# Modulating the first slice beside half of x, and summing two modulation vectors on VectorE from slice 3 on

## The chip, the core and the metric

The kernel runs on one core of one Trainium2 chip. The core has TensorE (PE in the profile; its weight loads are PEld), VectorE (DVE), ScalarE (ACT), GpSimd (POOL) and SyncE (SP), each with its own queue of instructions in order, and 16 DMA engines that all queues share. The metric is the device time of one execution in microseconds. Before the change its median is 1101.84 us in 3 runs (1101.22 to 1101.95).

## What is computed

One decoder block for 512 tokens of width 1024: a projection of the modulated and normalised input to gates, a spatial-gating branch and a Mamba-2 branch, then an output projection and an MLP. The change touches only the beginning, cut here to what matters:

```python
mod = (silu(c) @ w_mod + b_mod)          # one row of 6*1024
sh1, sc1, g1, sh2, sc2, g2 = split(mod, 6)
h = rms_norm(x) * (1.0 + sc1) + sh1      # 512 x 1024
proj = h @ w_in                          # 512 x 10272
u, v, z, xbc, dt_raw, gate_a, gate_b = split(proj, offs)
```

## The kernel before

All arithmetic is float32. A large product is three products of float32r halves: each operand is split into a rounded part H and a remainder L, and HH, HL and LH are summed in PSUM. One product of a 128x128 stationary tile with 128x512 moving columns is called a matmul below. ScalarE writes the H of a weight (a cast), VectorE the L (a subtraction).

h is kept transposed (channels in partitions, tokens in columns) in eight slices of 128 channels, slice k in hH[k] and hL[k]. The first stage is a loop over the slices (L420): as soon as slice k is there, its 896 columns of w_in (384 of u, 512 of v) are multiplied with it into seven PSUM banks that stay open for the whole loop: vps[0..3], one for each block of 128 tokens, and ups[0..2]. One slice takes 21 matmuls, three kinds (HH, HL, LH) for seven banks. The rest of the program, 14 times as long, follows: v's second half (v1), u, gates, the two branches, the output and the MLP.

What a slice needs ahead of that:

- **x** is loaded in eight halves of 128 tokens by 512 channels (xt[t][0] and xt[t][1]; in listings of the order of instructions x_66 to x_73, in the order t=0 first half, t=0 second half, t=1 first half, and so on). xstat(t) (L359) sums the squares of the two halves, one on ScalarE and one on VectorE; xn(t) (L371) scales 256 channels by 1/rms and transposes two slices' blocks on TensorE. For later slices xn_t (L349) transposes four blocks, and ScalarE copies them out of PSUM (xnT).
- **sh1 and 1+sc1 of the slice** come from mod_load(k) (L230), two loads of 512 KB on SyncE's queue, then mod_rows(k) (L312), eight small TensorE products of silu(c) with them, a copy to SBUF (mrow), mod_cols(k) (L323), two transposes and a reduction, and an addition of the bias. The result is mcol[k] (mc in the profile).
- **the modulation** writes hH[k] on ScalarE (mod_H, L377) and the same in float32 on GpSimd, for k=0 on VectorE (mod_f, L380); VectorE subtracts them to hL[k] (low, L107).
- **w_in's 896 columns** are loaded by start_load(k) (L247) and split by start_H and start_L (L341, L345).

Buffers set when loads may start: three for mod (rawt), four for w (wide). spin(n) (L272) is n matmuls of ones that nobody reads. There are two rings of PSUM banks, five "mm" and three "sx"; after the open banks have been given out one sx bank is left, which mod_rows, mod_cols and xn_t share in turn.

The engine order is that of the code for PE, ACT, DVE and SP in this stage (class InOrder). In the loop mod_rows(k+1) stands after the second of slice k's matmuls, mod_cols(k+1) after the seventh, xn_t(k+2) after the thirteenth:

```python
if n == (7 if k == 0 else 1) and k + 1 < KB:
    mod_rows(k + 1)
if n == (12 if k == 0 else 6) and k + 1 < KB:
    mod_cols(k + 1)
```

After the loop GpSimd issues loads of small vectors in a block that waits for pool_at (L454): dcol (d_skip), bsb (gm_bs) and wsr (gm_ws), used from vectors() (L515) and spatial() (L573) on.

Of the kernel before, what the change touches and what calls it, by code (L numbers as in the profile page):

```python
# [10 lines left out]
AF = mybir.ActivationFunctionType  # L11
ALU = mybir.AluOpType
# [3 lines left out]
P = 128  # L16
S = 512
D = 1024
NT = S // P
KB = D // P  # L20
# [3 lines left out]
MASKED = -30000.0  # L24
OU, OV, OZ, OX, OB, OC, ODT, OGA, OGB = 0, 1024, 2048, 4096, 6144, 7168, 8192, 8224, 9248
AHEAD = 2
SPIN = 16
POOL_L = {("ga", 0), ("ga", 1), ("gm", 0), ("ga", 2), ("wo", 1, 0), ("wo", 1, 1), ("f1", 0, 0), ("f1", 0, 1)}
NB = 43

# [2 lines left out]
def hybrid_block(ctx: ExitStack, tc: tile.TileContext, x, c, w_mod, b_mod, w_in, gm_norm_w, gm_ws,  # L33
# [3 lines left out]
    pool = nc.gpsimd  # L37
# [20 lines left out]
    pe, dve, act = InOrder(nc.tensor, True), InOrder(nc.vector, True), InOrder(nc.scalar, True)  # L58
    sp = InOrder(nc.sync, True)
# [15 lines left out]
    def blk(name, dt=F32, n=512):  # L75
        return big.tile([P, n], dt, tag="b", name=nm(name), bufs=NB)

    def small(name, n):
        return big.tile([P, n], F32, tag="sm", name=nm(name), bufs=16)

    def wide(name):
        return big.tile([P, 1024], F32, tag="cr", name=nm(name), bufs=4)
# [18 lines left out]
    def add(o, a, b):  # L101
        dve.tensor_tensor(o, in0=a, in1=b, op=ALU.add)

    def stt(o, a, s, b, op0, op1):
        dve.scalar_tensor_tensor(o, in0=a, scalar=s, in1=b, op0=op0, op1=op1)

    def low(L, src, H, eng=None):  # L107
        (eng or dve).tensor_tensor(L, in0=src, in1=H.bitcast(F32), op=ALU.subtract)  # L108
# [7 lines left out]
    mm, tr = pe.matmul, pe.transpose  # L116
# [71 lines left out]
    W = w_in[0]  # L188
# [32 lines left out]
    xt = [[blk("x"), blk("x")] for _ in range(NT)]  # L221

    def x_load(eng, t, j):
        eng.dma_start(xt[t][j], x[0, t * P:(t + 1) * P, j * 512:(j + 1) * 512])
# [9 lines left out]
            sp.dma_start(raw[:, j], w_mod[0][:, c0:c0 + P].rearrange("(k p) n -> p k n", p=P))  # L234
        return raw

    for t in range(NT):
        x_load(act, t, 0)
    x_load(sp, 0, 1)
    x_load(sp, 1, 1)  # L240
    sp.dma_start(crow, c.rearrange("a (r p) -> (a r) p", p=P))
    modraw = [mod_load(0)]
    x_load(sp, 2, 1)
    x_load(sp, 3, 1)
    C0 = OU + 640

    def start_load(k):  # L247
        raw = wide("w0")
        sp.dma_start(raw[:, 0:896], W[k * P:(k + 1) * P, C0:C0 + 896])
        return raw  # L250

    startraw = [start_load(0)]
    for k in range(1, KB):
        modraw.append(mod_load(k))
        startraw.append(start_load(k))
# [1 line left out]
    ones = const([P, P], "ones")  # L257
    dve.memset(ones, 1.0)
    ident = const([P, P], "ident")
# [12 lines left out]
    def spin(n):  # L272
        for _ in range(n):
            mm(spinps[:, 0:P], lhsT=ones, rhs=ones, start=True, stop=True)
# [22 lines left out]
    cact = const([P, KB], "cact")  # L297
# [6 lines left out]
    bm = const([P, KB, 2], "bm")  # L304
# [29 lines left out]
    def wide_pair(name):
        pair = [big.tile([P, KB, S], F32R, tag=f"hh{i}", name=nm(name), bufs=1) for i in range(2)]
        return pair, [pair[0][:, k, :] for k in range(KB)], [pair[1][:, k, :] for k in range(KB)]

    _, hH, hL = wide_pair("h")
    wstart = {}

    def start_H(k):  # L341
        wstart[k] = whl()
        act.copy(wstart[k][0][:, 0:896], startraw[k][:, 0:896])

    def start_L(k):  # L345
# [11 lines left out]
    rs = [small("rstd", 1) for _ in range(NT)]  # L357

    def xstat(t):  # L359
        sqacc(accx[t][:, 0:1], xt[t][0])  # L360
        dve.scalar_tensor_tensor(blk("junk"), in0=xt[t][1], scalar=1.0, in1=xt[t][1], op0=ALU.mult, op1=ALU.mult,
                                 accum_out=accx[t][:, 1:2])
        add(ssx[t], accx[t][:, 0:1], accx[t][:, 1:2])
        act.activation(sqx[t], ssx[t], AF.Sqrt, bias=epsc, scale=1.0 / D)

    def xscale(eng, t, c0, c1):
        o = xt[t][c0 // 512]
        eng.tensor_scalar(o[:, c0 % 512:c0 % 512 + c1 - c0], in0=o[:, c0 % 512:c0 % 512 + c1 - c0], scalar1=rs[t],
                          scalar2=None, op0=ALU.mult)

    def xn(t):  # L371
        dve.reciprocal(rs[t], sqx[t])
        xscale(dve, t, 0, 256)
        for k in range(2):
            xn_t(tps[k], k, t)

    def mod_H(k, xk, t0=0, t1=S):  # L377
        act.activation(hH[k][:, t0:t1], xk[:, t0:t1], AF.Identity, bias=mcol[k][:, 0:1], scale=mcol[k][:, 1:2])

    def mod_f(k, xk):  # L380
        hf = blk("h")
        at = (pool if k else dve).tensor_scalar(hf, in0=xk, scalar1=mcol[k][:, 1:2], scalar2=mcol[k][:, 0:1],
                                                op0=ALU.mult, op1=ALU.add)
        return hf, at.ins

    xstat(0)
    xstat(1)
# [1 line left out]
    xn(0)  # L389
    spin(3)  # L390
    xn(1)
    spin(6)
    mod_rows(0)
    spin(2)
    xstat(2)
    mod_cols(0)
    xscale(dve, 0, 256, 512)
    spin(2)
    xn(2)
    xscale(dve, 1, 256, 512)  # L400
    mod_H(0, tps[0], 0, 256)
    spin(4)
    xstat(3)
    wstart[0] = whl()
    pool.tensor_copy(wstart[0][0][:, 0:896], startraw[0][:, 0:896])
    xn(3)
    mod_H(0, tps[0], 256, 512)
    hf, _ = mod_f(0, tps[0])
    low(hL[0], hf, hH[0])
    act.copy(xnT[1], tps[1])  # L410
    start_L(0)
    for t in (0, 1, 2, 3):
        act.mul(xt[t][1], xt[t][1], rs[t])
    for t in (2, 3):
        xscale(dve, t, 256, 512)
    start_H(1)
    start_L(1)
    vps = [mm_bank() for _ in range(NT)]
    ups = [mm_bank(), sx_bank(), sx_bank()]
    for k in range(KB):  # L420
        WH, WL = wstart[k]
        H, L = hH[k], hL[k]
        banks = [(vps[t], t) for t in range(NT)] + [(ps, 4 + j) for j, ps in enumerate(ups)]
        steps = [(i, b) for i in range(3) for b in banks] if k < KB - 1 else [(i, b) for b in banks for i in range(3)]
        for n, (i, (ps, b)) in enumerate(steps):
            w, h = (WL if i == 2 else WH), (L if i == 1 else H)
            if b < 4:
                lhsT, rhs = h[:, b * P:(b + 1) * P], w[:, 384:896]
            else:
                lhsT, rhs = w[:, (b - 4) * P:(b - 3) * P], h  # L430
            mm(ps, lhsT=lhsT, rhs=rhs, start=k == 0 and i == 0, stop=k == KB - 1 and i == 2)
            if n == (7 if k == 0 else 1) and k + 1 < KB:
                mod_rows(k + 1)
            if n == (12 if k == 0 else 6) and k + 1 < KB:
                mod_cols(k + 1)
            if n == (17 if k == 0 else 12) and k + 2 < KB:
                tp = sx_bank()
                for t in range(NT):
                    xn_t(tp, k + 2, t)
        if k + 1 < KB:  # L440
            mod_H(k + 1, xnT[k + 1])
            hf, pool_at = mod_f(k + 1, xnT[k + 1])
        if k + 2 < KB:
            act.copy(xnT[k + 2], tp)
            start_H(k + 2)
        if k + 1 < KB:
            low(hL[k + 1], hf, hH[k + 1])
        if k + 2 < KB:
            start_L(k + 2)

    dve.on = act.on = sp.on = False

# [36 lines left out]
    vps = [mm_bank() for _ in range(NT)]  # L489
# [571 lines left out]
```

## Time and profile before

| what | value |
|---|---|
| median of 3 runs | 1101.84 us (1101.22 to 1101.95) |
| the profiled execution | 1104.26 us |
| its span, first to last instruction | 1102.6 us |
| TensorE busy | 1080.4 us, 98% of the span |
| VectorE, ScalarE, GpSimd busy | 642.1, 479.0, 192.8 us |
| first matmul of slice 0 | 20.69 us |
| first matmul of slice 1, of slice 7, of v1 | 29.27, 69.09, 73.85 us |

Times in the trace count from the span's start. The profiled execution is 1.66 us longer than its span and 2.42 us longer than the median. Matmul records overlap their successors, so the step from one start to the next (0.2275 us for 128x512) is the cost of one in a stream, not the duration that stands in the row. The granted clock of TensorE is 1.00 (2.4 GHz) or 0.50 (1.2 GHz).

### The profile page before, as it was taken

The page shows a single profiled execution, that of the slowest core. Times are in us where ns is not written, and L with a number is a line of the kernel's source. Part 1 is how long each engine was busy: PE and PEld are TensorE (multiplying, and loading weights), DVE is VectorE, ACT ScalarE, POOL GpSimd, SP SyncE. Part 2 cuts the span into 40 slices and gives each one's busy share as a digit, 9 for nine tenths or more (in the row PEclk, how much of TensorE's full clock was granted, in tenths as well). Part 3 has the DMA queues.
Part 4 walks back from the last instruction along what each step waited for, and adds up shares of the span by engine and source line. Part 5 has one row for each costly group of instructions (what it writes and reads, how often), then busy time and mean ns, then how long its engine had stood idle before and what let it go on. Part 6 is the DMA issues. An engine that isn't in the chain of part 4 may idle for free.

```text
span 1102.6 us, 13404 instructions
## 1 busy us (share of the span) xinstructions
PE 1080.4 (98%) x5386; PEld 895.1 (81%) x5386; DVE 642.1 (58%) x865; ACT 479.0 (43%) x629; POOL 192.8 (17%) x136
## 2 busy tenths in 40 slices
PE   7999998999999999999999999998999999999997
PEld 5778887888888888888888888888888888888886
DVE  4333599986787787778756544385443425444254
ACT  4356445337656566656446322233442112443222
POOL 0130663123422423423101000340000000000000
PEclk9999999999999999999999999999999999999999
DMA  9868256986332442532332324323323233333302
GB/s 301 248 124 154 77 170 231 315 262 201 118 112 82 148 127 81 157 120 90 125 115 77 115 78 142 105 77 96 115 78 113 81 110 90 101 101 109 110 6 77
DMA packets 122718, 141.65 MB, mean 128 GB/s; under 512 B 3712, under 2 KB 93888, under 8 KB 122656
## 3 DMA queue, kind: packets, MB, share of 16 engines
q1 hardware_dynamic: 120912, 137.54, 39.5%
q0 software_dynamic: 592, 1.16, 1.9%
q10 hardware_dynamic: 1152, 2.10, 0.5%
q8 instruction: 42, 0.69, 0.3%
q14 instruction: 20, 0.16, 0.0%
HBM read 138.54 MB, written 2.24 MB: 128 GB/s over the span
## 4 chain that ended last, share of the span: by engine, by line
PE 88%; DVE 6%; DMA 2%; ACT 1%; POOL 1%; issue 1%; SPq 0%; DVEq 0%; ACTq 0%; POOLq 0%
PE mm L49 73%; PE sx L49 15%; DMA mod<-in_w_mod_dram 1%; DVE xn L49 1%; DVE acc L49 1%; DVE e L49 1%; DMA cum<-cumd 1%; DVE xr L49 0%; POOL wL L108 0%; DVE q L49 0%; DMA crow<-in_c_dram 0%; ACT junk L49 0%; DVE ss L49 0%; DVE cum L49 0%; DVE s L49 0%
## 5 line engine op out<-in xcount | busy, mean ns | idle before, releaser
L49 PE MATMUL mm<-h,wH 128*128 128x512 f32 (+1 forms) x1712 | 521.1, 386 | 0.0
L49 PEld LDWEIGHTS mm<-h,wH 128*128 128x128 f32 x1712 | 312.5, 189 | 60.8 <-issue 2.7
L49 PE MATMUL mm<-h,wL 128*128 128x512 f32 (+1 forms) x856 | 327.6, 383 | 1.4 <-POOL wL L108 1.4
L49 DVE TENSOR_TENSOR wL<-raw,wH 128x1024 fp32r<-128x1024 f32 x154 | 200.0, 1302 | 209.1 <-ACT wH L49 208.4
L49 ACT CAST wH<-raw 128x1024 fp32r<-128x1024 f32 x170 | 177.6, 1048 | 289.7 <-PE mm L49 229.3
L49 PEld LDWEIGHTS mm<-h,wL 128*128 128x128 f32 x856 | 161.2, 188 | 33.9 <-POOL wL L108 1.6
L49 ACT ACT_TABLE_LOAD x64 | 82.1, 1283 | 7.3 <-issue 2.7
L49 DVE SCALAR_TENSOR_TENSOR cv<-mm,wcol,cv 128x511 f32<-128x511 f32 (+2 forms) x96 | 70.9, 742 | 11.4 <-ACT cv L49 10.8
L49 PE MATMUL mm<-wL,aH 128*128 128x512 f32 (+1 forms) x176 | 66.8, 380 | 0.0
L49 PE MATMUL mm<-wH,aH 128*128 128x512 f32 (+1 forms) x176 | 66.8, 380 | 0.0
L49 PE MATMUL mm<-wH,aL 128*128 128x512 f32 (+1 forms) x176 | 66.8, 379 | 0.0
L108 POOL TENSOR_TENSOR wL<-raw,wH 128x1024 fp32r<-128x1024 f32 x16 | 40.7, 2549 | 130.1 <-ACT wH L49 130.0
L710 POOL TENSOR_TENSOR cum<-cum,cumt 128x1024 f32<-128x1024 f32 x16 | 32.2, 2011 | 66.9 <-DMA cum<-cumd 29.6
L49 DVE TENSOR_TENSOR r<-r 128x512 f32<-128x512 f32 x32 | 22.0, 688 | 35.3 <-ACT r L49 35.3
L49 PE MATMUL mm<-wH,h 128*128 128x512 f32 x128 | 40.6, 403 | 0.1
L49 PE MATMUL mm<-y,wH 128*128 128x512 f32 x128 | 39.4, 389 | 0.0
L49 PEld LDWEIGHTS mm<-wH,aL 128*128 128x128 f32 x176 | 33.1, 188 | 6.2
L49 PEld LDWEIGHTS mm<-wL,aH 128*128 128x128 f32 x176 | 33.1, 188 | 6.0
L49 PEld LDWEIGHTS mm<-wH,aH 128*128 128x128 f32 x176 | 33.1, 188 | 5.9
L49 ACT ACTIVATE r<-mm 128x512 f32<-128x512 f32 x32 | 19.0, 595 | 39.2 <-PE mm L49 39.2
L49 DVE SCALAR_TENSOR_TENSOR acc<-mod,cact,acc 128x512 f32<-128x512 f32 x48 | 35.5, 790 | 0.5 <-DMA mod<-in_w_mod_dram 0.5
L49 PE MATMUL sx<-wL,aH 128*128 128x512 f32 (+1 forms) x96 | 35.7, 372 | 0.0
(228 smaller groups left out, 1511.7 us busy)
## 6 DMA issues: line engine op xcount, KB each, us to landing
raw<-in_w_ff_dram SPq DMA_DIRECT2D x32, 1024.0 KB, 5.1
raw<-in_w_in_dram SPq DMA_DIRECT2D x28, 1024.0 KB, 5.4
mod<-in_w_mod_dram SPq DMA_DIRECT2D x16, 1024.0 KB, 7.6
raw<-in_w_in_dram SPq DMA_DIRECT2D x18, 512.0 KB, 4.8
mod<-in_w_mod_dram SPq DMA_DIRECT2D x16, 512.0 KB, 7.1
cum<-cumd SPq DMA_DIRECT2D x16, 512.0 KB
raw<-in_w_branch_ssm_dram SPq DMA_DIRECT2D x8, 1024.0 KB, 5.6
raw<-in_w_branch_gm_dram SPq DMA_DIRECT2D x4, 1024.0 KB, 5.9
```

Source lines behind the costliest of these rows:

```text
L49: r = fn(*a, **k)
L108: (eng or dve).tensor_tensor(L, in0=src, in1=H.bitcast(F32), op=ALU.subtract)
L710: pool.tensor_tensor(cv, in0=cv, in1=ct, op=ALU.subtract)
```

## The change

- **Loads.** ScalarE's queue now loads both halves of the first two token blocks (before: the first half of all four) and then w of slice 0. SyncE's queue starts with c and the modulation of slice 0, then x of the last two blocks.
- **Slice 0 in halves of the tokens.** tps[0] holds the transposed blocks of tokens 0 to 255 for slices 0 and 1, tps[1] those of tokens 256 to 511 (before: one bank for each slice). first_half(0) modulates the first 256 tokens; four matmuls of slice 0 (HH and HL of vps[0] and vps[1]) stand ahead of xn(2), xn(3) and first_half(1). The other 17 follow.
- **Fewer spins** between: 3, 3, 3 after xn(0), xn(1), mod_rows(0), where there were 3, 6, 2, 2, 4.
- **From slice 3 on** (MOD_PE = 3) sh1 and sc1 are sums on VectorE: mod_acc runs over the eight k of w_mod, each 128x256, one tensor_scalar and seven scalar_tensor_tensor into one buffer; mod_sum then adds over the partitions on TensorE with two matmuls whose moving operand is one column of ones. For slices 1 and 2 mod_rows and mod_cols stay.
- **The float32 h** is written by ScalarE (a second activation) instead of GpSimd.
- **Order in a slice**: HH, then LH, then HL, so that hL is wanted last; xn_t stands after the second matmul.
- pool_at is now VectorE's last instruction of the stage.

```diff
-    for t in range(NT):
-        x_load(act, t, 0)
-    x_load(sp, 0, 1)
-    x_load(sp, 1, 1)
+    for t in (0, 1):
+        for j in range(2):
+            x_load(act, t, j)
     sp.dma_start(crow, c.rearrange("a (r p) -> (a r) p", p=P))
     modraw = [mod_load(0)]
-    x_load(sp, 2, 1)
-    x_load(sp, 3, 1)
...
+    startraw = [start_load(0, act)]
+    for t in (2, 3):
+        for j in range(2):
+            x_load(sp, t, j)
...
+    def mod_acc(k, j0, j1):
+        if j0 == 0:
+            accm[k] = blk("macc")[:, 0:256]
+        a = accm[k].rearrange("p (a b) -> p a b", a=2)
+        for j in range(j0, j1):
+            if j == 0:
+                dve.tensor_scalar(a, in0=modraw[k][:, :, j, :], scalar1=cact[:, 0:1], scalar2=None, op0=ALU.mult)
+            else:
+                stt(a, modraw[k][:, :, j, :], cact[:, j:j + 1], a, ALU.mult, ALU.add)
+
+    def mod_sum(k):
+        ps = sx_bank()
+        for a in range(2):
+            mm(ps[:, a:a + 1], lhsT=accm[k][:, a * P:(a + 1) * P], rhs=ones[:, 0:1], start=True, stop=True)
+        return ps
...
+    def first_half(i):
+        c = slice(256 * i, 256 * i + 256)
+        xk = tps[i][:, 0:256]
+        mod_act(hH[0][:, c], xk, 0)
+        dve.tensor_scalar(hf0[:, c], in0=xk, scalar1=mcol[0][:, 1:2], scalar2=mcol[0][:, 0:1], op0=ALU.mult,
+                          op1=ALU.add)
+        low(hL[0][:, c], hf0[:, c], hH[0][:, c])
...
+    for k in range(1, KB - 1):
+        more = k + 2 < KB
+        on_pe = k + 1 < MOD_PE
+        mains(k, 0, B7[:2])
+        if more:
+            tp = sx_bank()
+            for t in range(NT):
+                xn_t(tp, k + 2, t)
             act.copy(xnT[k + 2], tp)
+        mains(k, 0, B7[2:])
+        if not on_pe:
+            mod_acc(k + 1, 5, KB)
+        start_L(k + 1)
...
+            mains(k, 2, B7)
+            ps = mod_sum(k + 1)
+            mcol[k + 1] = small("mc", 2)
+            add(mcol[k + 1], ps[:, 0:2], bm[:, k + 1, :])
+            mains(k, 1, B7)
+        h_slice(k + 1)
+        if more:
             start_H(k + 2)
+            mod_acc(k + 2, 0, 5)
+        low(hL[k + 1], hfs[k + 1], hH[k + 1])
+    pool_at = dve.last
```

TensorE at the beginning, from mod_rows of slice 0 (the row with mod and cact) on; sx_139 is the spins' bank, mm_163 and mm_164 are tps, x_70 and x_72 the first halves of token blocks 2 and 3, h_161 is hH and h_162 is hL. Before:

```order
L49 MATMUL sx_225<-mod_84,cact_151 32x256 x8
L49 MATMUL sx_139<-ones 128x128 x2
L49 MATMUL sx_244<-ident,mrow_234 128x128 x2
L49 MATMUL sx_139<-ones 128x128 x2
L49 MATMUL mm_163<-ident,x_70 128x128
L49 MATMUL mm_164<-ident,x_70 128x128
L49 MATMUL sx_139<-ones 128x128 x4
L49 MATMUL mm_163<-ident,x_72 128x128
L49 MATMUL mm_164<-ident,x_72 128x128
L49 MATMUL mm_293<-wH_270,h_161 128x512
```

And now:

```order
L49 MATMUL sx_223<-mod_82,cact_151 32x256 x8
L49 MATMUL sx_139<-ones 128x128 x3
L49 MATMUL sx_243<-ident,mrow_232 128x128 x2
L49 MATMUL mm_256<-wH_250,h_161 128x512
L49 MATMUL mm_257<-wH_250,h_161 128x512
L49 MATMUL mm_256<-wH_250,h_162 128x512
L49 MATMUL mm_257<-wH_250,h_162 128x512
L49 MATMUL mm_164<-ident,x_70 128x128 x2
L49 MATMUL mm_164<-ident,x_72 128x128 x2
L49 MATMUL mm_256<-wL_251,h_161 128x512
L49 MATMUL mm_257<-wL_251,h_161 128x512
```

Four matmuls of slice 0 have moved ahead of the transposes of blocks 2 and 3, and no spins stand between those transposes.

VectorE in the loop, from the remainder of one slice (h_162, that is hL) to that of the next but one in the steady part; wL is the L of w, mrow and mc belong to the modulation. Before, one slice:

```order
L49 TENSOR_TENSOR h_162<-h_398,h_161 128x512
L49 TENSOR_TENSOR wL_402<-w_16_104,wH_401 128x896
L49 COPY mrow_417<-sx_408 128x256
L49 TENSOR_REDUCE mc_427<-sx_424 128x2
L49 TENSOR_TENSOR mc_429<-mc_427,bm 128x2
```

And now, macc being the sums of mod_acc:

```order
L49 TENSOR_TENSOR h_162<-h_394,h_161 128x512
L49 SCALAR_TENSOR_TENSOR macc_399<-mod_101,cact,macc_399 128x256 x3
L49 TENSOR_TENSOR wL_397<-w_16_104,wH_396 128x896
L49 TENSOR_TENSOR mc_433<-sx_430,bm 128x2
L49 TENSOR_SCALAR macc_448<-mod_106,cact 128x256
L49 SCALAR_TENSOR_TENSOR macc_448<-mod_106,cact,macc_448 128x256 x4
L49 TENSOR_TENSOR h_162<-h_443,h_161 128x512
```

The copy and the reduction are gone, and eight sums per slice stand in their place, five of them between the addition of mc and the next remainder.

ScalarE at the end of the stage, from hH of slice 6 to hH of slice 7 (h_161 in both); raw are the weights of v1. Before:

```order
L49 ACTIVATE h_161<-xnT_170,mc_588 128x512
L49 COPY xnT_171<-sx_596 128x512
L49 CAST wH_613<-w_24_124 128x896
L49 CAST wH_704<-raw_702 128x1024
L49 CAST wH_708<-raw_702 128x1024
L49 ACT_TABLE_LOAD
L49 ACTIVATE r_732<-epsc 128x1
L49 ACTIVATE h_161<-xnT_171,mc_641 128x512
```

And now:

```order
L49 ACTIVATE h_161<-xnT_170,mc_580 128x512
L49 ACTIVATE h_590<-xnT_170,mc_580 128x512
L49 CAST wH_592<-w_24_124 128x896
L49 CAST wH_679<-raw_677 128x1024
L49 CAST wH_683<-raw_677 128x1024
L49 ACT_TABLE_LOAD
L49 ACTIVATE r_707<-epsc 128x1
L49 ACTIVATE h_161<-xnT_171,mc_623 128x512
```

The copy of xnT has gone from between the two (it stands ahead of hH of slice 6 now), and the second activation, the float32 h, has come in; the casts for v1 and the table load stay ahead of hH of slice 7.

## Rows read from the trace of the kernel before

**Rows 1.** The page: busy time of each engine, and the chain that ended last.

```profile
PE 1080.4 (98%) x5386; PEld 895.1 (81%) x5386; DVE 642.1 (58%) x865; ACT 479.0 (43%) x629; POOL 192.8 (17%) x136
...
PE 88%; DVE 6%; DMA 2%; ACT 1%; POOL 1%; issue 1%; SPq 0%; DVEq 0%; ACTq 0%; POOLq 0%
```

**Rows 2.** One stretch: busy time of each engine, granted clock, DMA share, GB/s.

```profile
11.40:20.70 9.30, 6.90 (x65) 5.75 (x64) 4.01 (x16) 2.13 (x7) 0.93 (x1) 1.00 1.11 322
```

**Rows 3.** Timeline of VectorE, 0 to 22 us: start, duration, operation, idle before.

```profile
9.61 0.69 DVE L49 SCALAR_TENSOR_TENSOR junk<-x 128x512 f32<-128x512 f32 x1
...
11.40 0.35 DVE L49 TENSOR_SCALAR x<-x,rstd 128x256 f32<-128x256 f32 x1
15.43 0.43 DVE L49 COPY mrow<-sx 128x256 f32<-128x256 f32 x1 [3.68 <-PE sx L49]
...
16.84 0.16 DVE L49 TENSOR_TENSOR mc<-mc,bm 128x2 f32<-128x2 f32 x1
```

**Rows 4.** Timeline of SyncE's queue, 0 to 75 us: issues of loads.

```profile
9.61 0.33 SPq L49 DMA_DIRECT2D w<-in_w_in_dram  x1
...
37.67 0.99 SPq L49 DMA_DIRECT2D mod<-in_w_mod_dram  x2
...
44.39 0.99 SPq L49 DMA_DIRECT2D mod<-in_w_mod_dram  x2
```

**Rows 5.** Timeline of TensorE, 0 to 22 us.

```profile
14.29 1.07 PE L49 MATMUL sx<-mod,cact 128*32 128x256 f32 x16
...
20.69 1.76 PE L49 MATMUL mm<-wH,h 128*128 128x512 f32 x4
```

**Rows 6.** Timeline of TensorE, 28 to 76 us: first matmuls of slices and mod_rows.

```profile
29.27 0.62 PE L49 MATMUL mm<-wH,h 128*128 128x512 f32 x2
...
62.86 0.61 PE L49 MATMUL mm<-wH,h 128*128 128x512 f32 x2
63.40 1.07 PE L49 MATMUL sx<-mod,cact 128*32 128x256 f32 x16
...
69.09 0.61 PE L49 MATMUL mm<-wH,h 128*128 128x512 f32 x2
...
73.85 0.39 PE L49 MATMUL mm<-wH,h 128*128 128x512 f32 x1
```

**Rows 7.** VectorE's groups by form: count, busy us, mean ns, idle before.

```profile
L49 DVE TENSOR_TENSOR wL<-w,wH 128x896 fp32r<-128x896 f32 x8 | 8.7, 1092 | 7.8 <-ACT wH L49 7.8
...
L49 DVE TENSOR_TENSOR h<-h,h 128x512 fp32r<-128x512 f32 x8 | 5.5, 692 | 7.1 <-POOL h L382 7.1
...
L49 DVE TENSOR_TENSOR xr<-xr,r 128x256 f32<-128x256 f32 x2 | 0.8, 425 | 0.1
```

**Rows 8.** Timeline of VectorE, 154 to 175 us: dependent and independent neighbours.

```profile
154.87 0.68 DVE L49 TENSOR_TENSOR q<-s 32x512 f32<-32x512 f32 x1
155.58 0.41 DVE L49 TENSOR_SCALAR e<-q 32x512 f32<-32x512 f32 x1
...
169.73 4.05 DVE L49 SCALAR_TENSOR_TENSOR acc<-mod,cact,acc 128x512 f32<-128x512 f32 x6
```

**Rows 9.** Timeline of ScalarE, 54 to 76 us.

```profile
59.84 0.81 ACT L49 ACTIVATE h<-xnT,mc 128x512 fp32r<-128x512 f32 x1 [3.93 <-DVE mc L49]
...
61.70 0.94 ACT L49 CAST wH<-w 128x896 fp32r<-128x896 f32 x1
62.54 1.99 ACT L49 CAST wH<-raw 128x1024 fp32r<-128x1024 f32 x2
64.55 1.28 ACT L49 ACT_TABLE_LOAD   x1
```

**Rows 10.** Timeline of TensorE, 184 to 193 us.

```profile
188.06 0.47 PE L49 MATMUL sx<-m2H,onesr 128*128 128x512 f32 x1 [1.97 <-DVE dtt L49]
...
189.62 0.63 PE L49 MATMUL mm<-yaH,wH 128*128 128x512 f32 x1
190.05 0.63 PE L49 MATMUL mm<-yaL,wH 128*128 128x512 f32 x1
```

**Rows 11.** DMA issues, 0 to 90 us: count, KB each, median us from issue to landing.

```profile
mod<-in_w_mod_dram SPq DMA_DIRECT2D x16, 512.0 KB, 7.1
...
bsb<-in_gm_bs_dram POOLq DMA_DIRECT2D x2, 256.0 KB, 23.3
```

**Rows 12.** Timeline of VectorE, 100 to 118 us: first use of bsb.

```profile
114.46 0.75 DVE L49 SCALAR_TENSOR_TENSOR ya<-sx,cols,bsb 128x512 f32<-128x512 f32 x1 [1.25 <-PE sx L49]
```

More of the change, by code (lines that the diff above doesn't have):

```diff
@@ L26 @@
 AHEAD = 2
-SPIN = 16
+MOD_PE = 3
 POOL_L = {("ga", 0), ("ga", 1), ("gm", 0), ("ga", 2), ("wo", 1, 0), ("wo", 1, 1), ("f1", 0, 0), ("f1", 0, 1)}
@@ L235, in mod_load, with start_load @@
         return raw
-    for t in range(NT):
-        x_load(act, t, 0)
-    x_load(sp, 0, 1)
-    x_load(sp, 1, 1)
+    C0 = OU + 640
+    def start_load(k, eng=sp):
+        raw = wide("w0")
+        eng.dma_start(raw[:, 0:896], W[k * P:(k + 1) * P, C0:C0 + 896])
+        return raw
+    for t in (0, 1):
+        for j in range(2):
+            x_load(act, t, j)
     sp.dma_start(crow, c.rearrange("a (r p) -> (a r) p", p=P))
     modraw = [mod_load(0)]
-    x_load(sp, 2, 1)
-    x_load(sp, 3, 1)
[L245 to L252, printed above, removed]
+    startraw = [start_load(0, act)]
+    for t in (2, 3):
+        for j in range(2):
+            x_load(sp, t, j)
     for k in range(1, KB):
@@ L332, in mod_cols @@
         add(mcol[k], m, bm[:, k, :])
+    accm = {}
+    def mod_acc(k, j0, j1):
[12 more added lines that the diff above has]
+        return ps
     def wide_pair(name):
@@ L374, in xn, with mod_act, second @@
         for k in range(2):
[L375 to L384, printed above, removed]
+            o = k * 256 + t % 2 * P
+            tr(out=tps[t // 2][:, o:o + P], in_=xt[t][0][:, k * P:(k + 1) * P], identity=ident)
+    def mod_act(o, xk, k):
+        act.activation(o, xk, AF.Identity, bias=mcol[k][:, 0:1], scale=mcol[k][:, 1:2])
+    hf0 = blk("h")
+    def first_half(i):
[5 more added lines that the diff above has]
+        low(hL[0][:, c], hf0[:, c], hH[0][:, c])
+    def second(i):
+        act.copy(xnT[1][:, 256 * i:256 * i + 256], tps[i][:, 256:512])
     xstat(0)
@@ L391, in hybrid_block @@
     xn(1)
-    spin(6)
+    spin(3)
     mod_rows(0)
-    spin(2)
     xstat(2)
+    spin(3)
     mod_cols(0)
[L397 to L403, printed above, removed]
     wstart[0] = whl()
     pool.tensor_copy(wstart[0][0][:, 0:896], startraw[0][:, 0:896])
-    xn(3)
[L407 to L412, printed above, removed]
+    first_half(0)
@@ new lines, in hybrid_block, with mains @@
+    vps = [mm_bank() for _ in range(NT)]
+    ups = [mm_bank(), sx_bank(), sx_bank()]
+    def mains(k, i, banks):
+        WH, WL = wstart[k]
+        for b in banks:
+            w, h = (WL if i == 2 else WH), (hL if i == 1 else hH)[k]
+            if b < 4:
+                ps, lhsT, rhs = vps[b], h[:, b * P:(b + 1) * P], w[:, 384:896]
+            else:
+                ps, lhsT, rhs = ups[b - 4], w[:, (b - 4) * P:(b - 3) * P], h
+            mm(ps, lhsT=lhsT, rhs=rhs, start=k == 0 and i == 0, stop=k == KB - 1 and i == 1)
@@ L413, in hybrid_block @@
+    mains(0, 0, (0, 1))
+    mains(0, 1, (0, 1))
+    xstat(3)
+    start_L(0)
+    act.mul(xt[0][1], xt[0][1], rs[0])
+    act.mul(xt[1][1], xt[1][1], rs[1])
+    xn(2)
+    xn(3)
+    second(0)
+    first_half(1)
+    second(1)
+    mains(0, 2, (0, 1))
+    for t in (2, 3):
         act.mul(xt[t][1], xt[t][1], rs[t])
-    for t in (2, 3):
+    for t in range(NT):
         xscale(dve, t, 256, 512)
     start_H(1)
-    start_L(1)
-    vps = [mm_bank() for _ in range(NT)]
-    ups = [mm_bank(), sx_bank(), sx_bank()]
@@ L420, in hybrid_block @@
[L420 to L443, printed above, removed]
-            act.copy(xnT[k + 2], tp)
-            start_H(k + 2)
[L446 to L449, printed above, removed]
@@ new lines, in hybrid_block, with h_slice @@
+    B5 = (2, 3, 5, 6, 4)
+    mains(0, 0, B5)
+    mains(0, 2, B5[:2])
+    mod_rows(1)
+    mains(0, 2, B5[2:])
+    mod_cols(1)
+    start_L(1)
+    hfs = {}
+    def h_slice(k):
+        mod_act(hH[k], xnT[k], k)
+        hfs[k] = blk("h")
+        mod_act(hfs[k], xnT[k], k)
+    h_slice(1)
+    low(hL[1], hfs[1], hH[1])
+    tp = sx_bank()
+    for t in range(NT):
+        xn_t(tp, 2, t)
+    act.copy(xnT[2], tp)
+    mains(0, 1, B5)
+    start_H(2)
+    B7 = tuple(range(7))
+    for k in range(1, KB - 1):
[3 more added lines that the diff above has]
+        if more:
+            tp = sx_bank()
+            for t in range(NT):
+                xn_t(tp, k + 2, t)
+            act.copy(xnT[k + 2], tp)
+        mains(k, 0, B7[2:])
+        if not on_pe:
+            mod_acc(k + 1, 5, KB)
+        start_L(k + 1)
+        if on_pe:
+            mains(k, 2, B7[:2])
+            mod_rows(k + 1)
+            mains(k, 2, B7[2:])
+            mod_cols(k + 1)
+            mains(k, 1, B7)
+        else:
+            mains(k, 2, B7)
+            ps = mod_sum(k + 1)
+            mcol[k + 1] = small("mc", 2)
+            add(mcol[k + 1], ps[:, 0:2], bm[:, k + 1, :])
+            mains(k, 1, B7)
+        h_slice(k + 1)
+        if more:
+            start_H(k + 2)
+            mod_acc(k + 2, 0, 5)
+        low(hL[k + 1], hfs[k + 1], hH[k + 1])
@@ L451, in hybrid_block @@
+    pool_at = dve.last
+    mains(KB - 1, 0, B7)
+    for b in B7:
+        mains(KB - 1, 2, (b,))
+        mains(KB - 1, 1, (b,))
     dve.on = act.on = sp.on = False
```

## The prediction

> **What bounds the kernel now.** I read the page first: TensorE is busy 98% of the span and makes 88% of the chain that ended last [rows 1]. So only TensorE's own time, or its waiting ahead of the first real matmul, is worth anything. After the stage over the slices the change leaves every instruction of TensorE as it is, so I compare one number: when v1's first matmul starts, 73.85 us before [rows 6]. What that gains, the span should gain.
>
> The stage has three parts. The **head** ends with slice 0's first matmul at 20.69 [rows 5]; in the last 9.30 us of it TensorE is busy 6.90, in good part with spins [rows 2]. **Slice 0** lasts till 29.27. Slices 1 to 7 fill TensorE: slice 6 takes 69.09 - 62.86 = 6.23 us, slice 7, which has no modulation to prepare, 73.85 - 69.09 = 4.76, and slices 1 to 5 take (62.86 - 29.27)/5 = 6.72 [rows 6]. So mod_rows with mod_cols cost 6.23 - 4.76 = 1.47 us of TensorE for each slice, and xn_t 6.72 - 6.23 = 0.49.
>
> **The head.** Of the first two token blocks the last half to come is the fourth on ScalarE's queue. Before, the fourth half on that queue was there by 9.61, when SyncE could issue the w that waited for it [rows 4]. I keep 9.6: ahead of it lie the same three halves. VectorE squared a half at 9.61 before too, and had scaled block 1 at 11.40 + 0.35 = 11.75 [rows 3]; that stays. Before, spins then held mod_rows(0) back until 14.29 [rows 5]. Now the last transposes start about 11.8 and three spins follow (0.21 each at full clock): mod_rows(0) at 12.7. From its start to mc took 16.84 + 0.16 - 14.29 = 2.7 us [rows 3, 5], so mc is there at 15.3-15.4 and ScalarE's 256 columns (half of 0.81 plus a fixed part, 0.55, [rows 9]) end at 15.9: the **first matmul at 15.9** instead of 20.69.
>
> It doesn't go on from there. Behind those 256 tokens VectorE has, in order, h and hL of the half (0.43 each, from the 0.425 of 256 columns [rows 7]), the squares of the last half of x (0.69 [rows 3]), wL of slice 0 (1.09 [rows 7]), and two reciprocals and scalings (about 1.0): the scaling of block 3 ends at 15.9 + 0.86 + 0.69 + 1.09 + 1.0 = 19.5. Then transposes and ScalarE's second half: 20.4. TensorE has six matmuls (1.4 us) to do between 15.9 and 20.4. From 20.4 it has the other 15 of slice 0 (3.4), mod_rows(1) and mod_cols(1) with their short gaps (1.5, as above) and xn_t with a wait for the shared bank (0.7): **slice 1 starts at 26.0**, 3.3 earlier.
>
> That is at full clock. In the one place where this trace lets TensorE stand, 1.97 us ahead of 188.06, the granted clock soon fell to half, and a matmul's step became 190.05 - 189.62 = 0.43 instead of 0.2275 [rows 10]; the same rows go on for 3.4 us, in which 15 matmuls' time gave about 8, so one such stretch costs up to 1.6 us. The spins kept the head at 1.00 before [rows 2]. Now from 14.3 to 20.4 TensorE works about 2 of 6 us. I take one stretch at half clock where it has work: slice 1 at 27.6, a **gain of 1.7 us**; the bounds are none (3.3) and two (0.1).
>
> The Trainium skill (Trainium Kernel Development and Optimization, Key Constraints) says that loads issued from different queues run on the same 16 DMA engines and interleave, so that another queue saves issue time only. By that rule putting w on ScalarE's queue brings nothing earlier, and its traffic would hold up the modulation's or x's. The DMA engines are full here [rows 2], which agrees with it.
>
> **Slices.** Slice 1 keeps its modulation on TensorE. xn_t(3) now comes after two matmuls and must wait until ScalarE, after two activations (0.81 each [rows 9]), has copied the bank that xn_t(2) filled: **-0.25**.
>
> For slices 3 to 7 (prepared in slices 2 to 6) TensorE gives up 1.47 us and gets two products with one column. No such product is in the trace. It can't cost less than nothing, and not more than the eight of mod_rows (1.0, [rows 6]: 63.40 to the next matmul at 64.40). Each loads a 128x128 float32 weight in two passes; a spin does that and 128 columns in 0.21, so two are 0.43 at most: I take 0.43. Four slices (2 to 5) become 6.72 - 1.47 + 0.43 = 5.68, **4 x 1.04 = +4.2 us**, if nobody else is late.
>
> VectorE could be. Its row now: one product and seven sums of 256 columns, each sum waiting for the last. Independent sums of 512 columns run at 4.05/6 = 0.675; 256 columns fewer are 0.692 - 0.425 = 0.27 less; a dependent one starts 0.03 after the end (154.87 + 0.68 to 155.58) instead of 0.07 ahead of it [rows 7, 8]: 0.50 each. 0.38 + 7 x 0.50 + 0.69 (hL) + 1.09 (wL) + 0.16 (mc), less 0.07 at some five joints, is 5.5 us against 5.68. TensorE still sets the pace, by 0.2. Their inputs are there: mod loads of slices 6 and 7 were issued at 37.67 and 44.39 [rows 4], 7.1 us to landing [rows 11], so at 45 and 51.5; VectorE wants them at about 50 and 56. GpSimd has nothing beside it.
>
> Slice 6 would need 6.23 - 1.47 + 0.43 = 5.2. But from hH of slice 6 to hH of slice 7 ScalarE has 0.81 + 0.81 + 0.94 + 1.99 + 1.28 + 0.2 = 6.0, some 5.9 with overlaps [rows 9]; hH of slice 6 is ready some 0.4 ahead of need, so the slice takes about 5.5: **+0.7** instead of 1.04. Slice 7 stays.
>
> Sum: 1.7 - 0.25 + 4.2 + 0.7 = 6.3 us. v1 starts at 67.5; the span is 1102.6 - 6.3 = 1096.3, the profiled execution 1104.26 - 6.3 = 1098.0, and against the median 1101.84 - 6.3 = **1095.5**.
>
> **Rivals.**
> - *The clock stays up* (2.4 us of idle time in 9.3 did not lower it before [rows 2]): slice 1 at 26.0, gain 7.9, 1093.9. *Two stretches at half clock, or a late head*: gain 4.7, 1097.1.
> - *The rule about queues bites*: w's 448 KB go through the same engines while x and the modulation are still coming, at 322 GB/s [rows 2] 1.4 us. If the fourth half lands at 11.0 all of the head moves: 1096.9. This is what the page of the skill named above would make of it; that w stands behind the four halves on its own queue speaks against it.
> - *VectorE becomes the bound*. It decides as soon as a sum costs over 0.52. The upper bound is 512 columns with the dependence, 0.675 + 0.10 = 0.78: a slice of 7.4, four slices lose 2.8 and slice 6 loses 1.2, which makes -2.6 in all, 1104.4. Half way, at 0.65, slices take 6.5: 1099.8. Nothing was seen that makes 256 strided columns so dear.
> - *Slower*: GpSimd now issues bsb only after wsr has landed and been masked, where the two were issued together. bsb took 23.3 us [rows 11], most of it behind dcol's small packets. If it takes that again from about 95, it lands at 118, 10 us after VectorE wants it (114.46 - 6.3 = 108.2 [rows 12]); VectorE's weights' L parts wait behind that instruction, and TensorE for those. Slower from a loss over 6.3 us on; with all 10 us, 1105.5. Alone on its queue it should take some 4 us.
>
> **How the numbers follow.** Forecast 0.40; clock up 0.18; two stretches or a late head 0.17; queues 0.08; VectorE 0.10 (a third still faster, a third same, a third slower); bsb 0.04; the change doing nothing in the head and half in the slices, within 0.2%, 0.03. A difference of 0.2% (2.2 us) is about what a measurement of this kernel can tell from none. Faster 0.86, same 0.07, slower 0.07. The range leaves out the slow ends and a little at the fast one: 1092.5 (clock up and the two products nearly free, 1093.9 - 4 x 0.35) to 1099.8 (sums at 0.65).
>
> **What would show it.** First matmul of slice 0 near 16, slice 1 between 26 and 29, starts of slices 2 to 6 5.7 apart, of slices 6 and 7 5.5, v1 near 67.5. Half clock should show between 16 and 25. Sums of 0.45 to 0.5 with no wait of TensorE for macc; ScalarE, not VectorE, last ahead of slice 7. It is wrong if slices 3 to 6 wait for VectorE, if xn(0) waits for a half of x beyond 11 us, or if TensorE stands near 105 to 115 us.

## The result, and the profile after

| | median | ratio to before, 95% interval | v1's first matmul |
|---|---|---|---|
| before | 1101.89 us (1101.22 to 1102.64, 4 runs) | | 73.85 us |
| after | 1111.33 us (1110.54 to 1112.74, 4 runs) | 1.0087 [1.0069, 1.0104] | 83.35 us |

The changed kernel is 0.9% slower; the forecast was 0.6% faster. The profiled execution takes 1111.96 us, its span is 1110.2. The one number that the prediction followed carries the whole difference: v1's first matmul comes at 83.35 us instead of 73.85, 9.50 later, and the medians differ by 9.44. So the loss lies ahead of v1. (The two profiled spans differ by 7.6 us only: behind v1 the profiled execution of the kernel before took 1028.75 us and this one 1026.85; the former is 2.4 us above the median of its kernel.)

The timeline of TensorE of the changed kernel, 9 to 50 us (start, duration, operation, idle before), shows it in one row [rows 5, 6]:

```profile
17.17 0.70 PE L49 MATMUL mm<-wH,h 128*128 128x512 f32 x2 [1.36 <-ACT h L49]
...
20.50 1.15 PE L49 MATMUL mm<-ident,x 128*128 128x128 f32 x4 [1.65 <-DVE x L49]
...
29.06 0.63 PE L49 MATMUL mm<-wH,h 128*128 128x512 f32 x2
...
31.33 0.63 PE L49 MATMUL mm<-wL,h 128*128 128x512 f32 x2
43.34 1.93 PE L49 MATMUL sx<-mod,cact 128*32 128x256 f32 x16 [11.37 <-ACT xnT L49]
```

Slice 1 starts at 29.06 (before 29.27) and then TensorE stands for 11.37 us in the middle of it. What it waited for is in the chain of work between 16 and 50 us:

```profile
16.08 25.76 DMA w<-in_w_in_dram
41.84 0.02 issue
41.86 0.94 ACT wH L49
42.80 0.49 ACT xnT L49
43.34 1.93 PE sx L49 x16
```

A load of w that SyncE issued at 16.08 landed at 41.84. ScalarE's cast of it stood ahead of the copy of xnT, and mod_rows(2) wanted the bank which that copy frees. The stretches (busy us of PE, PEld, DVE, ACT, POOL, then granted clock, DMA share, GB/s) say what the DMA engines did meanwhile [rows 2]:

```profile
17.00:20.00 3.00, 1.43 (x4) 0.59 (x4) 2.80 (x7) 1.66 (x6) 0.14 (x1) 1.00 1.13 316
20.00:24.00 4.00, 3.50 (x10) 2.43 (x11) 2.51 (x10) 2.45 (x6) 0.00 (x0) 0.59 1.96 55
24.00:28.00 4.00, 3.74 (x30) 2.23 (x30) 1.55 (x6) 1.65 (x3) 0.00 (x0) 0.98 0.57 9
28.00:32.00 4.00, 3.96 (x19) 2.66 (x17) 1.25 (x2) 1.64 (x3) 0.00 (x0) 1.00 1.70 11
32.00:36.00 4.00, 0.00 (x0) 0.00 (x0) 0.00 (x0) 0.00 (x0) 0.00 (x0) 0.80 0.06 19
36.00:40.00 4.00, 0.00 (x0) 0.00 (x0) 0.00 (x0) 0.00 (x0) 0.00 (x0) 0.50 0.51 169
```

From 20 us on they were held and moved next to nothing: 55, 9, 11, 19 GB/s. (The shares, some over 1, can't be read closely here; the bytes can.) By queue, the DMA view of 16 to 44 us (packets, MB, share of 16 engines' time; then issues with KB and us to landing):

```profile
q0 software_dynamic: 244, 0.08, 57.7%
q1 hardware_dynamic: 4503, 3.07, 37.1%
...
dcol<-in_d_skip_dram POOLq DMA_DIRECT2D x2, 4.0 KB, 19.3
```

GpSimd's queue, with 0.08 MB in 28 us, held 57.7% of the engines' time. That is GpSimd's block of small vector loads, and its timeline shows that pool_at doesn't hold it any more:

```profile
11.35 0.93 POOL L426 CAST wH<-w 128x896 fp32r<-128x896 f32 x1 [8.52 <-DMA w<-in_w_in_dram]
12.22 0.20 POOL L523 MEMSET r<- 128x128 f32 x1
...
15.46 1.68 POOL L535 DMA_DIRECT2D dcol<-in_d_skip_dram  x2
59.69 0.91 POOL L542 DMA_DIRECT2D wsr<-in_gm_ws_dram  x1 [42.55 <-DVE wL L49]
```

Before, seven products (mod_f) of GpSimd stood ahead of the block, each waiting for its slice, and dcol went out at 70.66 us. pool_at was the last of them. GpSimd's timeline of the kernel before:

```profile
66.64 0.77 POOL L382 TENSOR_SCALAR h<-xnT,mc 128x512 f32<-128x512 f32 x1 [5.94 <-DVE mc L49]
67.35 0.21 POOL L456 MEMSET r<- 128x128 f32 x1
...
70.66 1.68 POOL L468 DMA_DIRECT2D dcol<-in_d_skip_dram  x2
```

Now the float32 h is written by ScalarE, GpSimd has no work in the loop, and pool_at names an instruction of VectorE. The block starts as soon as slice 0's w is cast, at 12.22 us. Being told to come after an instruction of VectorE held nothing on GpSimd; wsr alone waits, for the buffer that it goes into.

### The profile page after: what moved, and what is told of

Its sections match the earlier page's. It is cut to its first block, busy times and chain, and to the rows that moved or that the text cites. A ratio compares the mean times of both kernels' runs of the same rounds, so it can differ in the third digit from the quotient of the medians.

```text
span 1110.2 us, 13254 instructions
## 1 busy us (share of the span) xinstructions
PE 1078.3 (97%) x5300; PEld 895.8 (81%) x5300; DVE 655.1 (59%) x897; ACT 482.9 (43%) x637; POOL 186.3 (17%) x129
## 4 chain that ended last, share of the span: by engine, by line
PE 87%; DVE 6%; DMA 4%; ACT 1%; issue 1%; SPq 0%; POOL 0%; DVEq 0%; ACTq 0%
PE mm L49 74%; PE sx L49 13%; DMA w<-in_w_in_dram 2%; DMA mod<-in_w_mod_dram 2%; DVE xn L49 1%; DVE acc L49 1%; DVE e L49 1%; SPq L49 0%; POOL wL L108 0%; DVE xr L49 0%; DVE macc L49 0%; DVE q L49 0%; DVE ss L49 0%; ACT junk L49 0%; DVE s L49 0%
## 5 line engine op out<-in xcount | busy, mean ns | idle before, releaser
L49 DVE TENSOR_TENSOR wL<-raw,wH 128x1024 fp32r<-128x1024 f32 x154 | 196.3, 1278 | 206.6 <-ACT wH L49 206.3
```

The source lines that it names most:

```text
L49: r = fn(*a, **k)
```

## The experiments

The theory **T**: the loss is the block released at 12 us, above all dcol's packets, which hold the 16 DMA engines while w and the modulation of the next slices are wanted. The rivals: **R1**, the new order of the loads delays the later ones; **R2**, VectorE's sums keep the modulation buffers, and so the loads behind them; **R3**, half clock in the head.

### The block held on GpSimd

```diff
-    pool_at = dve.last
+    pool_at = pool.tensor_copy(small("mc", 2), hfs[KB - 1][:, 0:2]).ins
```

> The changed kernel, with GpSimd's block of vector loads held on GpSimd itself behind a tiny copy of slice 7's h, about where the last GpSimd product stood before. Theory T (the loss is the vector loads that run at 12 us and hold the DMA engines): no idle of TensorE between 31 and 43 us, slice 1 at about 29.1, slices 2 to 5 5.73 us each, v1's first matmul at about 69.2 instead of 83.4, and 1097.3 us (1096 to 1098.5). Rivals R1 (the new order of the x, w and modulation loads delays the later ones) and R2 (VectorE's sums keep the modulation buffers and so the loads): the stall stays, 1110 to 1112. R3 (half clock in the head): at most the 2.4 us of half clock after 43.3 change, 1108 to 1111.

Measured: 1098.82 us, ratio 0.9974 [0.9961, 0.9986]. The stall is gone: slice 1 starts at 29.03, slices 2 to 6 at 35.98, 41.68, 47.43, 53.16 and 58.90, slice 7 at 64.21. R1 and R2 fall, since their causes are all still there, and R3 too: the head still has its half clock (0.50 from 20 to 24 us). It is 1.5 us slower than T's number. The timelines of TensorE and of ScalarE of this kernel show where:

```profile
68.76 0.39 PE L49 MATMUL sx<-h,wH 128*128 128x512 f32 x1
70.83 0.50 PE L49 MATMUL mm<-wH,h 128*128 128x512 f32 x1 [1.69 <-ACT v L49]
```

```profile
69.24 1.04 ACT L49 CAST wH<-raw 128x1024 fp32r<-128x1024 f32 x1 [2.17 <-PE sx L49]
70.19 2.05 ACT L49 ACTIVATE v<-mm 128x512 f32<-128x512 f32 x4
```

The stage ends at 69.0 (T had v1 start at 69.2), but with the added instruction the scheduler placed a fourth weight cast of v1 ahead of the Gelu that frees vps[0], and that cast waits for a buffer that slice 7's last matmul frees. The 1.69 us belong to the experiment, not to the change.

### The kernel before, with the block early

```diff
+    early = pool.tensor_copy(wstart[0][0][:, 0:896], startraw[0][:, 0:896]).ins
...
-    with tc.issue_after(pool_at):
+    with tc.issue_after(early):
...
+    with tc.issue_after(pool_at):
         bsb = [blk("bsb"), blk("bsb")]
```

> The kernel before, with only the first part of GpSimd's block (clearing r, the loads of r, dtb, nega and dcol) ordered ahead of the slices' products on GpSimd, so that it is issued at 12 to 17 us as in the changed kernel. Theory T: a stall of TensorE in slice 1 or 2 on w, as in the changed kernel but shorter, since its slices take 6.7 us and not 5.7: 1108 to 1113 us. R1, R2, R3: none of their causes is in this kernel, 1101.5 to 1103.

Measured: 1113.71 us, ratio 1.0107 [1.0091, 1.0122]. The old kernel, with its old head and no sums, loses 11.8 us from the early loads alone. Its TensorE:

```profile
46.62 1.93 PE L49 MATMUL sx<-mod,cact 128*32 128x256 f32 x16 [10.13 <-DMA mod<-in_w_mod_dram]
```

The stall came as T said, though on a load of the modulation and not of w, and 0.7 us beyond T's range. So what makes the loss needs nothing of the change but the release of the block's first part.

### dcol alone: held, and loaded in rows

First the two dcol loads alone were put behind slice 7's h, the rest of the block left at 12 us.

> The changed kernel with the two dcol loads alone held behind slice 7's h; the other vector loads run at 12 us as in the changed kernel. If dcol's packets of 64 four-byte elements are what holds the DMA engines: within 1.5 us of the kernel with all of them held, 1097 to 1099. If the vector loads hold them in equal parts: 1102 to 1108. R1, R2, R3: 1110 to 1112.

Measured: 1103.73 us, ratio 1.0012 [1.0000, 1.0024]. By its number this is the case of equal parts; the trace says otherwise. The stall at 32 us is gone and v1 starts at 70.57, but the time is lost again behind it. Windows of this kernel and its waits between 76 and 115 us:

```profile
72.00:78.00 6.00, 6.00 (x28) 4.99 (x27) 1.79 (x2) 2.39 (x4) 0.00 (x0) 1.00 0.18 0
78.00:84.00 6.00, 6.00 (x28) 4.95 (x28) 1.78 (x2) 1.05 (x1) 0.00 (x0) 1.00 1.31 1
```

```profile
ACT wH L49 <- DMA raw<-in_w_in_dram: 11.0, 1, 11.0
...
PE sx L49 <- DVE wsT L49: 3.2, 1, 3.2
```

dcol, issued at 66.92, holds the engines again (0 and 1 GB/s), this time in front of v1's weights: ScalarE waits 11.0 us for one, VectorE's L part comes late, wsT stands behind it in VectorE's queue, and TensorE waits 3.2 us for wsT. With the whole block held, dcol went out at 68.57, behind other small loads, and no cast waited for a weight load: 204 GB/s were moved from 66 to 72 us, against 127 here. That a load got through ahead of dcol's packets there is inferred from this. So dcol held up what was behind it in this place too; this run convicts dcol of the stall but doesn't give its price. (Its trace has 64 packets of dcol with 8 KB, so 32 elements in a packet and not the 64 of the expectation.)

The other way is to leave everything at 12 us and change only dcol's form:

```diff
-        for j in range(2):
-            pool.dma_start(dcol[j * 64:(j + 1) * 64, :],
-                           d_skip[0].rearrange("(b j) -> j b", j=2)[j].partition_broadcast(64))
+        drow = const([P, 32], "drow")
+        pool.dma_start(drow, d_skip[0].partition_broadcast(P))
+        for j in range(2):
+            pool.tensor_copy(dcol[j * 64:(j + 1) * 64, :],
+                             drow[j * 64:(j + 1) * 64].rearrange("p (b j) -> p j b", j=2)[:, j])
```

> The changed kernel with one thing other: dcol is no longer gathered element by element by two loads, but a row of d_skip is loaded whole to all partitions and GpSimd copies its even and odd columns. All vector loads still run at 12 us. If dcol's packets alone make the stall: no idle of TensorE near 32 us, slice 1 at 28 to 29 us, steps of 5.73 us, v1's first matmul at 69 to 70, and 1097 us (1096 to 1098.5). If the other vector loads have a part in it: 1100 to 1106. If neither: 1110 to 1112.

Measured: 1098.11 us, ratio 0.9958 [0.9944, 0.9972]: 13 us less than the changed kernel by one load's form. Its stretches, and the same view of the queues from 16 to 44 us:

```profile
20.00:24.00 4.00, 3.67 (x11) 2.54 (x12) 2.55 (x9) 2.45 (x6) 0.39 (x2) 0.58 1.15 320
24.00:28.00 4.00, 3.74 (x31) 2.28 (x30) 1.52 (x5) 1.63 (x3) 0.00 (x0) 1.00 1.13 304
28.00:32.00 4.00, 3.99 (x24) 2.70 (x26) 2.18 (x3) 2.81 (x5) 0.00 (x0) 1.00 1.13 300
```

```profile
q0 software_dynamic: 224, 0.11, 1.7%
...
drow<-in_d_skip_dram POOLq DMA_DIRECT2D x1, 16.0 KB, 5.6
```

320, 304 and 300 GB/s where the changed kernel had 55, 9 and 11; GpSimd's queue holds 1.7% of the engines' time, not 57.7%, with more bytes. The other vector loads, released just as early, cost no stall.

The control is the kernel before with the same new form of dcol:

> The kernel before with dcol loaded in rows, nothing else. There dcol ran at 72 to 92 us, beside 76 GB/s of other loads. If no load of that stretch is urgent: within 1 us of the kernel before, 1101 to 1102.9. If dcol's packets cost time there too: faster by 1 to 4 us.

Measured: 1102.42 us, ratio 1.0000 [0.9992, 1.0009]. Where it stood before, dcol cost nothing that can be measured, though it held the engines there too. In the kernel before:

```profile
78.00:84.00 6.00, 6.00 (x28) 4.99 (x27) 1.23 (x1) 1.05 (x1) 0.00 (x0) 1.00 0.00 0
84.00:90.00 6.00, 6.00 (x28) 4.95 (x28) 1.23 (x1) 1.05 (x1) 0.00 (x0) 1.00 1.52 1
```

So the 76 GB/s of the expectation, a mean from 72 to 96 us, flowed ahead of 78 and behind 90 us, and TensorE, busy 6.00 of 6 us, had to wait for none of the loads that dcol held up. The form mattered only where such a load was urgent.

### The choice of queue for w

```diff
-    startraw = [start_load(0, act)]
+    startraw = [start_load(0)]
```

> The kernel with dcol in rows, and the w of slice 0 issued by SyncE behind the first modulation loads instead of by ScalarE. It prices the choice of queue for that load. By the traces its cast has about 3 us of room before the first matmul of slice 0, so no change from the kernel with dcol in rows, within 0.7 us (about 1097). If the queue decides when it lands and the head waits for it: slower by 1 to 2 us.

Measured: 1099.35 us, ratio 0.9963 [0.9950, 0.9975]; the interval overlaps that of the kernel with dcol in rows (0.9958). The medians lie 1.24 us apart, so a loss of 1 us can't be excluded by the times. The trace, of the fastest of the five executions (1096.00 us), shows none: slice 1 starts at 28.62 and v1 at 69.20 (28.89 and 69.55 with ScalarE's queue). No effect of that load's queue is seen, which is in keeping with the Trainium skill's rule on queues that the prediction cites. The loss that the rival attached to it didn't come either: VectorE starts on the fourth half of x at 9.83 us here and at 10.06 with ScalarE's queue, not at 11.0.

### What the two halves of the change are worth

More spins in the head, on the kernel with dcol in rows (4 more ahead of xn(0), 8 ahead of the first matmul of slice 0, 9 ahead of xn(2)):

> The kernel with dcol in rows, and more idle matmuls of TensorE in the head (4 more ahead of the first transposes, 8 ahead of the first matmul of slice 0, 9 ahead of the transposes of token tile 2), where it sat idle for 1.4 to 1.6 us ahead of the half-clock stretch at 20.7 us. If the idle is what the drop follows: no half clock between 16 and 25 us, slice 1 up to 1.6 us earlier, 1095.4 to 1096.5. If not: 1097 to 1097.8.

Measured: 1096.54 us, ratio 0.9942 [0.9930, 0.9954], the lowest median of all. The stretches of its head:

```profile
17.00:20.00 3.00, 2.95 (x23) 2.42 (x22) 2.83 (x9) 1.66 (x6) 0.00 (x0) 1.00 1.13 322
20.00:24.00 4.00, 3.81 (x29) 2.37 (x31) 2.43 (x8) 2.71 (x7) 0.38 (x2) 1.00 1.15 322
```

TensorE is busy 2.95 of 3 us ahead of 20, and the granted clock stays 1.00 (2.4 GHz) where it was 0.58 without them (1.00 and 0.68 in the pair without sums below). Slice 1 starts at 27.56 instead of 28.89, v1 at 68.01 instead of 69.55. The two intervals overlap, so the times alone would not tell the gain from none; the traces show it.

Then the sums were taken out (MOD_PE = 8: the modulation of all slices on TensorE), with the block held, with dcol in rows, and with rows and spins:

> The changed kernel with all vector loads held, and with the modulation of every slice on TensorE (MOD_PE 8), so that VectorE's sums are gone. It prices them: T: steps of slices 2 to 5 near 6.7 us instead of 5.7, 4.2 us in four of them and up to 1.2 in the step of slice 6, 1101.5 to 1103. R2: the sums held the loads, so without them it is faster than with them, under 1097.

> The kernel with dcol in rows, and the modulation of every slice on TensorE: what is left of the change is the head alone. From the traces so far: slice 1 at 28.9, then 6.95, four slices of 6.73, 6.3 and 4.84 make v1's first matmul 73.9, as in the kernel before: 1101 to 1103. If the head is worth the 1.7 us of the forecast: 1100.2. If the slices' part is worth less than the traces say, it stays below 1100.

> The same with the more idle matmuls in the head: the head alone without its half clock. Slice 1 at 27.6, v1's first matmul 1.3 us earlier than without them: 1100 to 1101.5. If the idle matmuls are worth nothing on the median: the same as without them, 1101 to 1103.

| dcol in rows, and | median | ratio, 95% interval | slice 1 | v1 |
|---|---|---|---|---|
| sums, few spins | 1098.11 | 0.9958 [0.9944, 0.9972] | 28.89 | 69.55 |
| sums, more spins | 1096.54 | 0.9942 [0.9930, 0.9954] | 27.56 | 68.01 |
| no sums, few spins | 1103.53 | 1.0006 [0.9997, 1.0015] | 29.34 | 74.28 |
| no sums, more spins | 1102.30 | 0.9993 [0.9983, 1.0002] | 28.21 | 73.18 |

With the block held and no sums it was 1105.12 us (1.0027 [1.0014, 1.0039]), 6.3 above the same with sums; that is more than the 5.4 (4.2 + 1.2) expected at most, and 1.0 of it is a later head in that run (slice 1 at 30.07 against 29.03). R2 expected the opposite sign. The two kernels without sums and with dcol in rows came out 0.5 and 0.8 us above their ranges; by its number the second is the case in which the spins are worth nothing on the median. The sums are worth 5.4 us with few spins by medians (1103.53 - 1098.11) and 4.7 by v1's start. The head alone is worth nothing that can be measured. The spins are worth 1.2 to 1.6 by medians, with overlapping intervals, and 1.1 to 1.5 by v1's start.

## Why the prediction was wrong, point by point

**The failed step is one sentence: "GpSimd has nothing beside it."** It put the wait for loads behind GpSimd's block at nothing, without a reason. The part on the change followed the removed products of GpSimd only as work that ScalarE now does. It didn't ask what stood behind them in GpSimd's queue. Those products, with their waits, were all that held the block of loads back; the part on the kernel before says that the block waits for pool_at, the part on the change only that pool_at has moved to VectorE, and the prediction names no row for what then holds the block. The orders shown ahead of the prediction are those of TensorE, VectorE and ScalarE; in GpSimd's, the one that mattered, the clearing of r stands directly behind slice 0's cast. What the runs showed in its place: GpSimd had the block beside it from 12.22 us on, and the w that slice 2 needed took 25.76 us to land, where the prediction reckoned with 7.1 for the loads of the modulation. With dcol in rows the changed kernel takes 1098.11 us and not 1111.33, so the missing term is 13.2 us.

**The slower rival** looked at the same block and priced one load of it, bsb, from the row with 23.3 us to landing [rows 11]. It even named dcol's small packets as the reason of those 23.3 us. It took them as a cost to bsb alone, at 95 us, and not as a cost to every load on the 16 engines, at 20 us. The row that shows it stood in the view of rows 11, of the kernel before:

```profile
dcol<-in_d_skip_dram POOLq DMA_DIRECT2D x2, 4.0 KB, 18.6
```

18.6 us for 4 KB, beside 7.1 for 512 KB of the modulation. In the changed kernel bsb, issued from 68.35 on, lands in 3.8 us, long ahead of its use at 123.75. So the direction had a chance of 0.07, and none of it for the reason that came.

**The head: +1.7 forecast, +0.2 came** (29.27 to 29.06; 0.4 with dcol in rows). Not even that can be told from none: the head of the kernel before ended at 28.84 in the run with dcol in rows, and the seven traces of the changed head with few spins have 28.62 to 30.07. Its stations were each late: the fourth half of x at 9.92 instead of 9.6, mod_rows(0) at 13.66 instead of 12.7 (the sum put the last transposes at 11.8 and left out that three spins stand ahead of them too; they came at 12.62, with three more spins behind them), the first matmul at 17.17 instead of 15.9, the transposes of block 2 at 20.50 with the half clock that the forecast had. With more spins slice 1 came at 27.56, against 27.6 forecast, but then with no half clock: the head is 1.3 us (28.89 against 27.6, at half clock) to 1.6 us (27.56 against 26.0, at full clock) longer than the sum made it, and that term is mis-sized whichever clock it gets. Most of it is there by the first matmul (16.98 against 15.9 with dcol in rows).

**Slice 1: -0.25 forecast.** It takes 35.86 - 28.89 = 6.97 us with dcol in rows, 0.25 over 6.72. Right, and most of it by the wait that was forecast: ScalarE's copy ends at 28.91 + 0.57 = 29.48 and xn_t(3) starts at 29.53, 0.64 behind the slice's start, where slice 2 has 0.47.

**Slices 2 to 5: 5.68 forecast, 5.70 to 5.75 measured** where nothing disturbs them. The two products with one column take 53.63 - 53.27 = 0.36 us, not 0.43; the sums follow each other at 0.51, not 0.50. The rows of the changed kernel, TensorE and then VectorE of the kernel with the block held:

```profile
53.27 0.50 PE L49 MATMUL sx<-ones,macc 128*128 128x1 f32 x4
53.63 1.19 PE L49 MATMUL mm<-wH,h 128*128 128x512 f32 x4
```

```profile
40.68 2.05 DVE L49 SCALAR_TENSOR_TENSOR macc<-mod,cact,macc 128x256 f32<-128x256 f32 x4
42.65 0.69 DVE L49 TENSOR_TENSOR h<-h,h 128x512 fp32r<-128x512 f32 x1
43.25 1.52 DVE L49 SCALAR_TENSOR_TENSOR macc<-mod,cact,macc 128x256 f32<-128x256 f32 x3
```

VectorE did not become the bound, except in one slice (below). **Slice 6: 5.5 forecast**, 5.43 in the changed kernel. Right, with the bound that was named: ScalarE runs without a gap from hH of slice 6 to hH of slice 7 (71.88 to 77.56), and slice 7 starts at 78.43, when that hH is done. (With the block held it is 5.31, but there the table load stands behind hH of slice 7.) From slice 1 to v1's start the sums gave (76.92 - 30.07) - (70.83 - 29.03) = 5.05 us with the block held, and (74.28 - 29.34) - (69.55 - 28.89) = 4.28 with dcol in rows, where slice 5 lost 0.4 (below). Forecast 4.2 + 0.7 = 4.9: **the larger term of the sum was right**, and lay under a loss of 13 us that had no term.

**The clock.** One stretch of half clock between 16 and 25 us was forecast, and one came, at 20.7 to 24.2. Its price was put at up to 1.6 us; without it slice 1 starts 1.1 to 1.3 us earlier. The prediction knew one place where TensorE stands; the trace of the kernel before has more: 4.13 us ahead of 749.00 (0.50 behind it) and 2.45 ahead of 6.08 (1.00 behind it). The changed kernel has a second stretch, 0.80 and then 0.50 from 32 us on in the stretches above; it begins inside the stall. Slice 1 takes 49.62 - 29.06 = 20.56 us there, against 6.97 with dcol in rows: 11.37 of the difference is the stall, and the half clock behind it is in the rest (mod_rows(2) takes 1.86 us, against 1.00).

## What to carry to other kernels

Work taken off an engine was also what held back the instructions behind it in its queue: list what comes up to the front, its loads included, and ask from which row it is known that something else still holds it. An order asked for between two engines held nothing here; take it to hold only where a wait is there to be seen. And a load is judged by the DMA time that it takes, not by its bytes: here two gathers of 4 KB were the most expensive loads of the stage.

## What the runs showed of the hardware

**A gather of small elements held the DMA engines.** By the profile's shares, in the 28 us from 16 to 44, GpSimd's queue held 0.577 x 16 x 28 = 258 us of engine time with 244 packets, and most of it is dcol, 2048 elements of 4 bytes: with dcol in rows 224 packets held 0.017 x 16 x 28 = 8 us. So dcol cost about 250 us of engine time by this estimate, 0.12 us an element and 16 us on each of the 16 engines; where it goes alone (dcol held, 66.9 to 92 us) the same view gives 0.677 x 16 x 25.1 = 272 us in 64 packets. The 16 us agree with the time without bytes, from 20 to 36 us. Whether the size of the elements makes the price or their number, no run separates. The Trainium skill (DMA: Bandwidth & Descriptors, Rules for kernel authors) says that a last dimension that is not contiguous becomes one descriptor for each element, and to rearrange it; no run counts the descriptors, but rearranging it paid, 13 us, and the traces put the price on it.

**A GpSimd instruction made a VectorE instruction nearly three times as long.** Slice 5 took 59.24 - 53.07 = 6.17 us with dcol in rows, where the others took 5.72 to 5.75. GpSimd masks wsr then, for 1.09 us, and VectorE's three sums beside it take 0.87 longer:

```profile
55.06 1.09 POOL L599 TENSOR_SCALAR_AFFINE_SELECT wsr<-wsr 128x1024 f32<-128x1024 f32 x1 [8.20 <-DMA wsr<-in_gm_ws_dram]
```

```profile
54.56 2.39 DVE L49 SCALAR_TENSOR_TENSOR macc<-mod,cact,macc 128x256 f32<-128x256 f32 x3
```

Three sums that took 1.52 us above take 2.39 here; the longest sum is 1.351 us, against a median of 0.485. With the block held the mask runs at 96.54, no sum is longer than 0.490 us, and slice 5 takes 5.74. The Trainium skill (SBUF — State Buffer, Who interferes with whom) says that a VectorE instruction with two SBUF inputs and a GpSimd instruction that reads SBUF exclude each other through a shared port: the sums read two tiles, and the trace agrees. This is a second, smaller cost of releasing GpSimd's block, some 0.4 us; it wasn't tried by itself.
